# A fourth seven-product pair in the last two up chunks, and ten prepared pairs spread over seven chunks

## The chip, the cores and the metric

One core of one Trainium2 chip runs the whole layer in one launch. The metric is device time in microseconds (us), the median of several executions. TensorE is called PE here, VectorE DVE, ScalarE ACT, GpSimd POOL; SP is SyncE, which in this kernel only issues DMAs.

## The reference

A decoder layer for 256 tokens of width 2048, in float32. The last third of it is what the change touches:

```python
h = _rmsnorm(x, norm_mlp_pre[layer])
u = jnp.square(jax.nn.relu(h @ w_up[layer]))          # 2048 -> 8192
x = x + _rmsnorm(u @ w_down[layer], norm_mlp_post[layer])   # 8192 -> 2048
```

Ahead of it stand an input projection, two kinds of causal attention and an output projection.

## The kernel before

**Three matmuls for a product.** Every float32 operand is split in two parts: ACT writes `hi`, the value rounded to the type in which PE multiplies, and DVE writes `lo`, what is left (`lo = raw - hi`). A product is three matmuls of 128 rows by 512 columns: hi by hi, lo by hi, hi by lo. Weights come from HBM into a ring of five `raw` buffers (SP issues those DMAs), are split there into a ring of eight `hi` and eight `lo` buffers, and are consumed in the order in which they were planned; a split is written into each engine's program 7 tiles ahead of its use on PE.

**Chunks and steps.** `h @ w_up` runs in eight chunks `j` = 0 to 7 of 1024 columns. The table `UP_STEPS` lists the steps of a chunk. `k8` is a plain step: one tile of 128 rows of the weight, for both blocks of 128 tokens and both halves of 512 columns, 4 products or 12 matmuls. `w1` and `p2` take a pair of such tiles at once (pair 1 is k2 and k3) by Strassen's scheme in Winograd's form, with seven products, 21 matmuls, where two plain steps have eight products, 24 matmuls. For that, sums of the weight's four quarters are needed (`t` and `u`) and sums of the left operand's quarters (`s`, one set for a pair, the same for all chunks; the list `sums`).
- In a `w` step DVE makes `t` and `u` (three instructions, L360, L364, L365) from `ab`, a buffer of two tiles that GpSimd's queue fills (L378). They stand in DVE's program two tiles ahead of the pair's own splits. There is one buffer `ab`. In chunk 7, `w` pairs after the first load through `raw` instead (`raw_w`).
- In a `p` step the two sums were made beforehand by DMAs that add in HBM (`prepare`, ten pairs, early in the program); they are read back through the buffer `tu` by GpSimd's queue (chunks 1 to 4) or as two more `raw` tiles by SP (later chunks). DVE makes no sums there.

**Left sums.** `left_sums` makes `s` of pairs 0 to 3 during chunk 0. Pairs 0 to 2 are kept in `st`; pair 3 in `st2`, whose memory becomes `uT10` at the end of chunk 5. So chunks 1 to 5 use four pairs, chunks 6 and 7 three.

**The end of a chunk.** Seven products fill the four sums of a chunk (`acc_u`) and four more banks (`m1`, `m6`, `m7`, `m5`). After the last pair, `close` combines those into the four quarters of `c`: one ACT instruction (L1086), four on DVE (L1089). Two plain steps (k14, k15) follow on PE. Then, for each of the four quarters, `up_evac` adds `c` to `acc_u` on DVE (L979), ACT writes `r = relu(...)` (L983), PE transposes `r` in four pieces (`rt`, L301) and ACT squares the result into `uT` (L1001). The instruction streams are recorded in the order in which a planned clock (`Flow`) reaches them; the numbers behind `yield` are waits on that planned clock. So the yields in `up_evac` set behind how many matmuls of the next chunk the transposes stand in PE's program, which PE runs in order. "The end of chunk 3" is this sequence for chunk 3; its transposes stand among the matmuls of chunk 4.

After chunk 7 come two chunks of `u @ w_down`, mostly of the same two kinds of steps. They use `c` as a second load buffer.

Of the kernel before, what the change touches and what calls it, by code (L numbers as in the profile page):

```python
# [18 lines left out]
F32 = mybir.dt.float32  # L19
F32R = mybir.dt.float32r  # L20
# [6 lines left out]
P = 128  # L27
# [18 lines left out]
CW = 1024  # L46
# [51 lines left out]
NUP = FF // CW  # L98


def steps_of(text):

    return [(s[0], int(s[1:])) for s in text.split()]


UP_STEPS = {0: [("k", k) for k in range(KD)]}
for _j in range(1, 6):
    UP_STEPS[_j] = steps_of("k8 k9 k10 k11 p0 k12 w1 k13 p2 w3 k14 k15")
for _j in range(6, NUP):
    UP_STEPS[_j] = steps_of("k6 k7 k8 k9 k10 w0 k11 k12 w1 k13 w2 k14 k15")  # L110
SCALED = {j: range(8) for j in range(1, NUP)}
PREP = [(j, k) for j in UP_STEPS for w, k in UP_STEPS[j] if w == "p"]
D_PREP = (50.0, 24.0, 12.0)
# [151 lines left out]
def layer(nc, tc, io):  # L265
# [9 lines left out]
    dram = tc.alloc_tile_pool(name="dram", bufs=1, space=bass.MemoryType.DRAM)  # L275
# [69 lines left out]
    late = {}  # L345
# [599 lines left out]
    for ns in ((0, 1), (2,), (3,)):  # L945
# [4 lines left out]
        for c, b, acc in proj(mixT, [ch_o[n] for n in ns], f"o{ns[0]}", order, heads_done):  # L950
            n = ns[c]
# [23 lines left out]
    def up_evac(j, b, i, acc, order, more=None):  # L975

        if more is not None:
            yield 0.2
            nc.vector.tensor_tensor(out=acc, in0=acc, in1=more, op=OP.add)  # L979
            yield 1.8 if 4 <= j < 10 else 2.4  # L980
        yield UP_STEP * order
        r = late["up"].tile([P, 512], F32, tag="r", bufs=2, name=f"r{j}_{b}")
        nc.scalar.activation(r, acc, AF.Relu, scale=rstd2[b])  # L983
        yield D_UP if j > 1 else 2 * D_UP
        t = bank(i, f"rt{j}_{b}")
        for k in range(4):
            transpose(t[:, k * P:(k + 1) * P], r[:, k * P:(k + 1) * P])
        if j not in uT:
            if j in (12, 13):
                t2 = late["ab"][:, (j - 12) * CW:(j - 11) * CW]  # L990
            elif j in (8, 9):
                if j == 8:
                    late["uT8"] = late["up"].tile([P, 2 * CW], F32, tag="uT8", bufs=1, name="uT8")
                t2 = late["uT8"][:, (j - 8) * CW:(j - 7) * CW]
            elif j == 10:
                t2 = late["up"].tile([P, CW], F32, tag="uT10", bufs=1, name="uT10")
            else:
                tag = {"tag": "T", "bufs": 2} if j > 13 else {}
                t2 = late["up"].tile([P, CW], F32, name=f"uT{j}", **tag)
            uT[j] = t2.rearrange("p (k s) -> p k s", k=4)  # L1000
        nc.scalar.activation(uT[j][:, :, b * P:(b + 1) * P], t.rearrange("p (k s) -> p k s", k=4), AF.Square)  # L1001
# [29 lines left out]
        tt(out=qs[:, 3], in0=fs[:, 2], in1=qs[:, 2], op=OP.subtract)  # L1031

    sums = []

    def left_sums(kp):

        up, k, tt = late["up"], 2 * kp, nc.vector.tensor_tensor
        f, q = [late["c"][:, i * 512:(i + 1) * 512] for i in (2 * (kp % 2), 2 * (kp % 2) + 1)]
        hs = [t[:, k:k + 2, :].rearrange("p k s -> p (k s)") for t in hT]
        cuts = [(slice(i * S, (i + 1) * S), gcol[:, 8 + k + i:9 + k + i]) for i in range(2)]  # L1040
        for c, g in cuts:
            nc.scalar.activation(f[:, c], hs[0][:, c].bitcast(F32), AF.Copy, scale=g)
        yield 1.5
        for c, g in cuts:
            nc.vector.scalar_tensor_tensor(out=f[:, c], in0=hs[1][:, c].bitcast(F32), scalar=g, in1=f[:, c],
                                           op0=OP.mult, op1=OP.add)
        four_sums(q, f)
        sp, i0 = (late["st"], 2 * kp) if kp < 3 else (late["st2"], 2 * kp - 6)
        st = [sp[:, i * 512:(i + 1) * 512] for i in (i0, i0 + 1)]
        yield 3.0  # L1050
        for t, x in ((hs, f), (st, q)):
            nc.scalar.activation(t[0], x, AF.Copy)
        yield 1.5
        for t, x in ((hs, f), (st, q)):
            tt(out=t[1], in0=x, in1=t[0].bitcast(F32), op=OP.subtract)
        sums.append([[t[:, i * P:(i + 1) * P] for t in st] for i in range(4)])
        yield 0.5

    def some_sums(kps, after=0.0):
        yield after  # L1060
        for kp in kps:
            yield from left_sums(kp)
# [29 lines left out]
    def closing():  # L1092
        return [late["c"][:, i * 512:(i + 1) * 512] for i in range(4)]
# [3 lines left out]
    for j in range(FF // CW):  # L1097
# [9 lines left out]
        for t, b in order:  # L1107
            what, k, tiles = steps[t]
            if (j, t, b) == (0, 8, 0):
                flow.finish(*res)  # L1110
                late["po"].release()
                mix.release()
                late["up"] = pool("up", "right")
                late["st"] = late["up"].tile([P, 3 * CW], F32R, tag="st", bufs=1, name="st")
                for n in ("ab", "c"):
                    late[n] = late["up"].tile([P, 2 * CW], F32, name=n)
                late["st2"] = late["up"].tile([P, CW], F32R, tag="uT10", bufs=1, name="st2")
                late["tu"] = late["up"].tile([P, 2 * CW], F32, tag="uT8", bufs=1, name="tu")
                flow.start(some_sums((0, 1)))
                flow.start(some_sums((2, 3), 18.0))  # L1120
            if (j, t, b) == (FF // CW - 1, 4, 0):
                weights.limit -= 1
                u_next = split_u(0, 0)
            if what != "k":
                flow.until(lambda: len(sums) > k)
            if what == "k":
                w = weights.get(tiles[0])
                h_done(k, b)
                for n in range(2):
                    c = slice(n * 512, (n + 1) * 512)  # L1130
                    three(accs[b, n], [tok(hT[x], k, b) for x in range(2)], [w[x][:, 0, c] for x in range(2)], t == 0, t == len(steps) - 1)
                    if t == len(steps) - 1:
                        evac.append(flow.start(up_evac(2 * j + n, b, at[b, n], accs[b, n], 0.75 * (2 * b + n),
                                                       more[b, n] if j else None)))
                    flow.pump()
                if b == NB - 1:
                    weights.free(tiles[0])
                continue

            pairs = [s[1] for s in steps if s[0] != "k"]  # L1140
            first, last = k == pairs[0], k == pairs[-1]
            if first:
                m = {n: bank(i, f"m{n}_{j}") for n, i in zip((1, 6, 7, 5), free)}
            blocks = [[tok(hT[x], 2 * k + kk, bb) for x in range(2)] for kk, bb in ((0, 0), (1, 0), (1, 1))]
            seven_products(tiles, (blocks, sums[k]), accs, m, first, last)
            if last:
                more = close(closing(), m)
        free = [at[bn] for bn in PARTS]
    u_last = evac[-4:]
    up = late["up"]  # L1150
# [212 lines left out]
```

## Time and profile before

| | |
|---|---|
| median of 3 runs | 1045.58 us (1045.51 to 1045.67) |
| the profiled execution | 1045.31 us, of which the span is 1043.4 us |
| PE | busy 1033.9 us, 99% of the span; 99% of the chain that ended last |
| DVE, ACT, POOL | busy 79%, 61%, 10% |
| granted PE clock | 0.998 |
| up chunks 1 to 7 | about 400 to 701 us of the span |

The span is counted from the first to the last instruction; 1.9 us lie around it. A busy PE in this profile says that matmuls follow each other, and not at which rate; the rate is read from the starts of the matmuls. In a timeline each row is a start, a length, an engine, a line, the operation with its output and inputs, and in brackets how long the engine was idle before it and what ended that.

### The profile page before, as it was taken

How to read it: one execution, taken by the hardware profiler on the slowest of the kernel's cores; microseconds unless marked ns; L12 is line 12 of the kernel's file. 1: busy time of each engine (PE TensorE's matmuls, PEld its weight loads, DVE VectorE, ACT ScalarE, POOL GpSimd, SP SyncE). 2: the span in 40 equal slices, each digit the busy share in tenths (PEclk: the TensorE clock that was granted, in tenths of full speed). 3: DMA queues.
4: the chain of work that ended last, by engine and by line, in shares of the span. 5: the costliest groups of instructions: out<-in, count | busy, mean ns of one | idle time of the engine just before them, and what ended most of it. 6: DMA issues, size and time to landing. Idle time of an engine off the chain costs nothing.

```text
span 1043.4 us, 13587 instructions
## 1 busy us (share of the span) xinstructions
PE 1033.9 (99%) x4832; PEld 862.2 (83%) x4832; DVE 820.7 (79%) x1096; ACT 640.3 (61%) x862; POOL 103.8 (10%) x165
## 2 busy tenths in 40 slices
PE   9999999999999999999999999999999999999996
PEld 7888889888888888888888888888888888888885
DVE  7766537567547669988889788888999899999994
ACT  7674436565445558666766666666667566766761
POOL 0011111112001010010100000000000001112100
PEclk9999999999999999999999999999999999999999
DMA  9999879699878286756766666468888859789962
GB/s 337 353 300 281 211 202 320 203 251 295 238 217 262 95 343 215 270 204 232 264 210 235 211 216 198 152 223 296 300 275 310 284 185 334 263 306 321 365 220 81
DMA packets 93716, 262.90 MB, mean 252 GB/s; under 512 B 8785, under 2 KB 12881, under 8 KB 92241
## 3 DMA queue, kind: packets, MB, share of 16 engines
q1 hardware_dynamic: 70480, 187.99, 52.1%
q0 software_dynamic: 22304, 72.89, 24.5%
q10 hardware_dynamic: 864, 1.16, 0.3%
q8 instruction: 38, 0.62, 0.2%
q14 instruction: 30, 0.24, 0.1%
HBM read 245.22 MB, written 40.37 MB: 274 GB/s over the span
## 4 chain that ended last, share of the span: by engine, by line
PE 99%; DMA 0%; DVE 0%; ACT 0%; DVEq 0%; POOL 0%; issue 0%; ACTq 0%
PE acc_u L297 25%; PE y L297 25%; PE acc_o L297 8%; PE m L297 7%; PE md L297 6%; PE acc_qk L297 4%; PE acc_v L297 4%; PE acc_ckv L297 2%; PE acc_ukv L297 2%; PE acc_q L297 2%; PE acc_cq L297 2%; PE acc_k L297 2%; PE acc_uq L297 2%; PE rt L301 1%; PE y L1237 1%; PE sc_b L297 1%
## 5 line engine op out<-in xcount | busy, mean ns | idle before, releaser
L308 DVE TENSOR_TENSOR lo<-raw,hi 128x1024 fp32r<-128x1024 f32 (+3 forms) x234 | 262.0, 1137 | 86.6 <-ACT hi L307 85.5
L307 ACT ACTIVATE hi<-raw 128x1024 fp32r<-128x1024 f32 (+3 forms) x234 | 228.2, 988 | 83.9 <-DMA raw<-in_w_in 16.0
L297 PE MATMUL acc_u<-hi,hT_hi 128*128 128x512 f32 x356 | 141.8, 398 | 0.0
L297 PE MATMUL y<-hi,uhi 128*128 128x512 f32 x358 | 139.8, 391 | 0.0
L297 PE MATMUL y<-hi,ulo 128*128 128x512 f32 x358 | 139.5, 390 | 0.0
L297 PE MATMUL y<-lo,uhi 128*128 128x512 f32 x358 | 139.5, 390 | 0.0
L297 PE MATMUL acc_u<-hi,hT_lo 128*128 128x512 f32 x356 | 139.3, 391 | 0.0
L297 PE MATMUL acc_u<-lo,hT_hi 128*128 128x512 f32 x356 | 139.0, 391 | 0.0
L312 DVE SCALAR_TENSOR_TENSOR lo<-raw,gcol,hi 128x1024 fp32r<-128x1024 f32 x72 | 90.7, 1281 | 17.8 <-ACT hi L311 17.6
L311 ACT ACTIVATE hi<-raw,gcol 128x1024 fp32r<-128x1024 f32 x72 | 81.9, 1149 | 20.9 <-DMA raw<-in_w_up 12.9
L297 PEld LDWEIGHTS y<-hi,ulo 128*128 128x128 f32 x358 | 67.2, 188 | 14.1
L297 PEld LDWEIGHTS y<-lo,uhi 128*128 128x128 f32 x358 | 67.3, 188 | 13.8
L297 PEld LDWEIGHTS acc_u<-hi,hT_lo 128*128 128x128 f32 x356 | 66.8, 188 | 14.3 <-DVE hT_lo L308 0.2
L297 PEld LDWEIGHTS y<-hi,uhi 128*128 128x128 f32 x358 | 67.2, 188 | 13.7
L297 PEld LDWEIGHTS acc_u<-lo,hT_hi 128*128 128x128 f32 x356 | 67.0, 188 | 13.0
L297 PEld LDWEIGHTS acc_u<-hi,hT_hi 128*128 128x128 f32 x356 | 67.0, 188 | 12.8
L297 PE MATMUL m<-hi,st 128*128 128x512 f32 x156 | 56.5, 390 | 0.0
L308 DVE TENSOR_TENSOR lo<-st_down,hi 128x1024 fp32r<-128x1024 f32 x46 | 55.1, 1219 | 0.8 <-ACT hi L307 0.8
L297 PE MATMUL acc_o<-hi,mixT_hi 128*128 128x512 f32 x128 | 51.9, 405 | 0.0
L307 ACT ACTIVATE hi<-st_down 128x1024 fp32r<-128x1024 f32 x46 | 48.2, 1051 | 5.7 <-PE y L297 5.1
L297 PE MATMUL acc_o<-hi,mixT_lo 128*128 128x512 f32 x128 | 50.2, 393 | 0.0
L297 PE MATMUL acc_o<-lo,mixT_hi 128*128 128x512 f32 x128 | 50.0, 391 | 0.0
(341 smaller groups left out, 2093.4 us busy)
## 6 DMA issues: line engine op xcount, KB each, us to landing
raw<-in_w_up SPq DMA_DIRECT2D x86, 512.0 KB, 4.6
raw<-in_w_down SPq DMA_DIRECT2D x82, 512.0 KB, 5.7
raw<-in_w_in SPq DMA_DIRECT2D x55, 512.0 KB, 7.0
raw<-in_w_out SPq DMA_DIRECT2D x32, 512.0 KB, 7.4
ab<-in_w_up POOLq DMA_DIRECT2D x28, 512.0 KB, 5.1
ab_down<-in_w_down POOLq DMA_DIRECT2D x24, 512.0 KB, 7.2
sums<-in_w_up SPq DMA_DIRECT2D x20, 512.0 KB, 6.9
tu<-sums POOLq DMA_DIRECT2D x8, 1024.0 KB, 5.3
```

The source lines that it names most:

```text
L297: nc.tensor.matmul(out, a, b, start=start, stop=stop)
L301: nc.tensor.transpose(out, a, ident)
L307: nc.scalar.activation(hi, src, AF.Copy)
L308: nc.vector.tensor_tensor(out=lo, in0=src, in1=hi.bitcast(F32), op=OP.subtract)
L311: nc.scalar.activation(hi, src, AF.Copy, scale=g)
L312: nc.vector.scalar_tensor_tensor(out=lo, in0=src, scalar=g, in1=hi.bitcast(F32), op0=OP.mult, op1=OP.subtract)
L1237: nc.tensor.matmul(out, a[x], w[z], start=False, stop=(x, z) == (1, 0), skip_group_check=True)
```

## The change

1. `UP_STEPS`: chunks 4 and 5 have `w0` where they had `p0`. Chunks 6 and 7 had plain steps k6 and k7 and pairs `w0 w1 w2`; now they have the same list as chunks 4 and 5, with four pairs `w0 w1 p2 w3`. So there are 28 pairs instead of 26, and still ten prepared ones: two in each of chunks 1 to 3 and one in each of chunks 4 to 7.
2. The left sums of pair 3 are written to HBM (`st_kept`) by GpSimd's queue after they are made, and in chunks 6 and 7 read back by SP's queue before the step k11 into the memory of `c`, which is free between the last addition of one chunk and the `close` of its own. `c` becomes a tile with a tag, taken anew for each of these uses.
3. In `up_evac` the wait before `r` is 3.2 instead of 2.4 for the two halves of chunk 7.

```diff
-for _j in range(1, 6):
+for _j in range(1, 4):
     UP_STEPS[_j] = steps_of("k8 k9 k10 k11 p0 k12 w1 k13 p2 w3 k14 k15")
-for _j in range(6, NUP):
-    UP_STEPS[_j] = steps_of("k6 k7 k8 k9 k10 w0 k11 k12 w1 k13 w2 k14 k15")
+for _j in range(4, NUP):
+    UP_STEPS[_j] = steps_of("k8 k9 k10 k11 w0 k12 w1 k13 p2 w3 k14 k15")
...
-            yield 1.8 if 4 <= j < 10 else 2.4
+            yield 1.8 if 4 <= j < 10 else 3.2 if j > 13 else 2.4
...
+    st_kept = dram.tile([P, CW], F32, name="st_kept")
+
+    def new_c(name, dt=F32):
+        return late["up"].tile([P, 2 * CW], dt, tag="c", bufs=1, name=name)
+
+    def parts_of(st):
+        return [[st[:, w * 512 + i * P:w * 512 + (i + 1) * P] for w in range(2)] for i in range(4)]
...
+        if kp == 3:
+            yield 8.0
+            nc.gpsimd.dma_start(out=st_kept, in_=sp.bitcast(F32))
...
+            if j > 5 and (t, b) == (3, 0):
+                late["st2"] = new_c(f"st2_{j}", F32R)
+                nc.sync.dma_start(out=late["st2"][:, :CW].bitcast(F32), in_=st_kept)
+                sums[3] = parts_of(late["st2"])
...
             if last:
+                if j > 5:
+                    late["c"] = new_c(f"c_{j}")
                 more = close(closing(), m)
```

In `up_evac`, `j` counts halves of 512 columns: 4 to 9 are chunks 2 to 4, 14 and 15 chunk 7.

The program moves as follows at three places. First, DVE's program at the end of chunk 3, before; `lo207` to `lo212` are the splits of k14 and k15 of chunk 3 and of k8 to k11 of chunk 4, `lo213` and `lo214` those of the first two tiles of chunk 4's pair 0.

```order
L312 SCALAR_TENSOR_TENSOR lo210_4789<-raw210_4786,gcol_69,hi210_4788 128x1024
L312 SCALAR_TENSOR_TENSOR lo211_4801<-raw211_4798,gcol_69,hi211_4800 128x1024
L312 SCALAR_TENSOR_TENSOR lo212_4813<-raw212_4810,gcol_69,hi212_4812 128x1024
L1089 TENSOR_TENSOR c_3574<-m6_3_4613,c_3574 128x512
L1089 TENSOR_TENSOR c_3574<-m7_3_4614,c_3574 128x512
L1089 TENSOR_TENSOR c_3574<-m5_3_4615,c_3574 128x512
L1089 TENSOR_TENSOR c_3574<-c_3574,m7_3_4614 128x512
L308 TENSOR_TENSOR lo213_4832<-raw213_4829,hi213_4831 128x512
L308 TENSOR_TENSOR lo214_4850<-raw214_4847,hi214_4849 128x1024
L979 TENSOR_TENSOR acc_u3_00_4501<-acc_u3_00_4501,c_3574 128x512
```

The same place after the change (the lines of the file are 10 further down from `close` on).

```order
L312 SCALAR_TENSOR_TENSOR lo210_4792<-raw210_4789,gcol_69,hi210_4791 128x1024
L360 TENSOR_TENSOR t4_0_4801<-ab_3574 128x1024
L364 TENSOR_TENSOR u4_0_4802<-t4_0_4801,ab_3574 128x512
L365 TENSOR_TENSOR u4_0_4802<-u4_0_4802,ab_3574 128x512
L312 SCALAR_TENSOR_TENSOR lo211_4809<-raw211_4806,gcol_69,hi211_4808 128x1024
L312 SCALAR_TENSOR_TENSOR lo212_4821<-raw212_4818,gcol_69,hi212_4820 128x1024
L1099 TENSOR_TENSOR c_3575<-m6_3_4615,c_3575 128x512
L1099 TENSOR_TENSOR c_3575<-m7_3_4616,c_3575 128x512
L1099 TENSOR_TENSOR c_3575<-m5_3_4617,c_3575 128x512
L1099 TENSOR_TENSOR c_3575<-c_3575,m7_3_4616 128x512
L308 TENSOR_TENSOR lo213_4836<-ab_3574,hi213_4835 128x512
L308 TENSOR_TENSOR lo214_4852<-ab_3574,hi214_4851 128x1024
```

The three instructions that make the sums of chunk 4's pair 0 now stand ahead of chunk 3's `close` and first addition; the same happens at the end of chunk 4. At the ends of chunks 5 and 6 they stood there already.

Second, PE's program where the first transposes of chunk 3 stand, before.

```order
L297 MATMUL acc_u4_10_4870<-hi209_4779,hT_lo_2923 128x512
L297 MATMUL acc_u4_11_4871<-hi209_4779,hT_hi_2922 128x512
L297 MATMUL acc_u4_11_4871<-lo209_4780,hT_hi_2922 128x512
L297 MATMUL acc_u4_11_4871<-hi209_4779,hT_lo_2923 128x512
L301 MATMUL rt6_0_4891<-ident_94,r6_0_4880 128x128 x4
L297 MATMUL acc_u4_00_4868<-hi210_4788,hT_hi_2922 128x512
```

And after.

```order
L297 MATMUL acc_u4_10_4872<-hi209_4782,hT_lo_2923 128x512
L297 MATMUL acc_u4_11_4873<-hi209_4782,hT_hi_2922 128x512
L297 MATMUL acc_u4_11_4873<-lo209_4783,hT_hi_2922 128x512
L297 MATMUL acc_u4_11_4873<-hi209_4782,hT_lo_2923 128x512
L301 MATMUL rt6_0_4895<-ident_94,r6_0_4884 128x128 x4
L297 MATMUL acc_u4_00_4870<-hi210_4791,hT_hi_2922 128x512
```

They stand behind the 12 matmuls of k8 in both. The same holds at the end of chunk 4 (12 and 12); at the ends of chunks 5 and 6 it is 15 and 15, at the end of chunk 7 it was 15 and is 18. PE's whole program has six matmuls fewer.

Third, SP's program in chunk 6 after the change: `raw265` is k12, `raw270` k13, `raw271` to `raw274` the four tiles of the prepared pair 2.

```order
L189 DMA raw260_5558<-in_w_up 128x1024
L189 DMA raw265_5674<-in_w_up 128x1024
L1132 DMA st2_6_5700<-st_kept_3328 128x1024
L189 DMA raw270_5757<-in_w_up 128x1024
L189 DMA raw271_5769<-in_w_up 128x512
L189 DMA raw272_5787<-in_w_up 128x1024
L189 DMA raw273_5801<-sums6_2_78 128x1024
L189 DMA raw274_5813<-sums6_2_78 128x1024
```

The new load stands in the middle of the weights' queue, which it did not have before; in chunk 7 it stands likewise between the loads of k12 and k13.

More of the change, by code (lines that the diff above doesn't have):

```diff
@@ L1114, in layer @@
                 late["st"] = late["up"].tile([P, 3 * CW], F32R, tag="st", bufs=1, name="st")
-                for n in ("ab", "c"):
-                    late[n] = late["up"].tile([P, 2 * CW], F32, name=n)
+                late["ab"], late["c"] = late["up"].tile([P, 2 * CW], F32, name="ab"), new_c("c")
                 late["st2"] = late["up"].tile([P, CW], F32R, tag="uT10", bufs=1, name="st2")
```

## The prediction

> **What bounds the kernel now.** I read the page's totals first, then the chain that ended last, then the timelines of DVE, ACT and PE around the ends of chunks, since only there does PE wait for a result that is made late. The totals and the chain's shares:
>
> ```profile
> PE 1033.9 (99%) x4832; PEld 862.2 (83%) x4832; DVE 820.7 (79%) x1096; ACT 640.3 (61%) x862; POOL 103.8 (10%) x165
> ...
> PE 99%; DMA 0%; DVE 0%; ACT 0%; DVEq 0%; POOL 0%; issue 0%; ACTq 0%
> ```
>
> PE is the chain from start to end. So time changes in two ways only: by the number of matmuls on PE, and by stalls of PE that come or go. The chain in order of time, at the ends of chunks 3, 4 and 5 (start, length, what):
>
> ```profile
> 523.19 8.16 PE acc_u L297 x36
> ...
> 565.92 8.16 PE acc_u L297 x36
> 574.09 0.44 PE rt L301 x4
> 574.52 2.09 PE acc_u L297 x9
> ...
> 608.66 8.84 PE acc_u L297 x39
> 617.50 0.50 PE rt L301 x4
> 618.00 2.08 PE acc_u L297 x9
> ```
>
> The 36 matmuls behind a chunk's last pair (24 of k14 and k15, 12 of the next chunk's first step) take 8.16 us without a gap: 0.2267 us each. At the end of chunk 5 there are 39, and the four transposes take 0.50 instead of 0.44: PE waited 0.06 us for `r` there. At the other ends shown it did not. How near `r` came is in the timelines. DVE at the end of chunk 3:
>
> ```profile
> 514.86 1.23 DVE L308 TENSOR_TENSOR lo<-t,hi 128x1024 fp32r<-128x1024 f32 x1 [1.30 <-ACT hi L307]
> 516.00 6.13 DVE L312 SCALAR_TENSOR_TENSOR lo<-raw,gcol,hi 128x1024 fp32r<-128x1024 f32 x5
> 522.36 1.28 DVE L312 SCALAR_TENSOR_TENSOR lo<-raw,gcol,hi 128x1024 fp32r<-128x1024 f32 x1 [0.22 <-ACT hi L311]
> 523.56 2.28 DVE L1089 TENSOR_TENSOR c<-m,c 128x512 f32<-128x512 f32 x3
> 525.87 0.69 DVE L1089 TENSOR_TENSOR c<-c,m 128x512 f32<-128x512 f32 x1
> 526.48 1.82 DVE L308 TENSOR_TENSOR lo<-raw,hi 128x512 fp32r<-128x512 f32 x2
> 528.21 1.89 DVE L979 TENSOR_TENSOR acc_u<-acc_u,c 128x512 f32<-128x512 f32 x3
> ```
>
> At 514.86 DVE had waited for ACT, so it held no backlog. From there it works through six splits, the close and two splits to the first addition at 528.21. ACT and PE at the same place:
>
> ```profile
> 528.94 0.69 ACT L983 ACTIVATE r<-acc_u,rstd_pre 128x512 f32<-128x512 f32 x1 [1.93 <-DVE acc_u L979]
> ...
> 531.19 0.60 PE L301 MATMUL rt<-ident,r 128*128 128x128 f32 x4
> ```
>
> `r` ends at 529.63, the transposes' turn on PE comes at 531.19: 1.56 us to spare.
>
> **The matmuls removed.** Two pairs (one each in chunks 6 and 7) go from two plain steps, 24 matmuls, to seven products, 21: six fewer, at 0.2267 us 1.36 us less. All of it lies on the chain. The trace knows no other price for a matmul in this stage, so this term has hardly a range.
>
> **The sums ahead of the close, chunks 3 and 4.** Because chunks 4 and 5 now begin with `w0`, DVE makes its sums ahead of the close. Their price stands where the same three instructions run now, for pair 1 of chunk 4:
>
> ```profile
> 531.74 1.22 DVE L360 TENSOR_TENSOR t<-ab 128x1024 f32<-128x1024 f32 x1
> 532.99 0.69 DVE L364 TENSOR_TENSOR u<-t,ab 128x512 f32<-128x512 f32 x1
> 533.72 0.69 DVE L365 TENSOR_TENSOR u<-u,ab 128x512 f32<-128x512 f32 x1
> 534.33 1.22 DVE L308 TENSOR_TENSOR lo<-tu,hi 128x1024 fp32r<-128x1024 f32 x1
> ```
>
> From 531.74 to 534.33 they hold DVE for 2.59 us, more than the 1.56 us to spare. What the whole sequence then takes shows at the end of chunk 5, which has these sums ahead of the close already:
>
> ```profile
> 600.33 1.23 DVE L308 TENSOR_TENSOR lo<-t,hi 128x1024 fp32r<-128x1024 f32 x1 [1.30 <-ACT hi L307]
> ...
> 607.37 1.22 DVE L360 TENSOR_TENSOR t<-ab 128x1024 f32<-128x1024 f32 x1
> ...
> 611.15 2.28 DVE L1089 TENSOR_TENSOR c<-m,c 128x512 f32<-128x512 f32 x3
> ...
> 615.87 1.89 DVE L979 TENSOR_TENSOR acc_u<-acc_u,c 128x512 f32<-128x512 f32 x3
> ...
> 616.60 0.69 ACT L983 ACTIVATE r<-acc_u,rstd_pre 128x512 f32<-128x512 f32 x1 [4.12 <-DVE acc_u L979]
> ...
> 617.34 0.66 PE L301 MATMUL rt<-ident,r 128*128 128x128 f32 x4
> ```
>
> From the start of the last pair's `lo<-t` at 600.33 to the transposes at 617.34 it is 17.01 us, and 17.07 with the 0.06 that they were late. That row has the same idle time before it (1.30, ended by ACT) as the row at 514.86, so both begin without a backlog. Applied to chunk 3: 514.86 + 17.07 = 531.93, while PE arrives at 531.19: PE stalls 0.74 us. At the end of chunk 4:
>
> ```profile
> 557.59 1.23 DVE L308 TENSOR_TENSOR lo<-t,hi 128x1024 fp32r<-128x1024 f32 x1 [1.30 <-ACT hi L307]
> ...
> 572.08 0.67 ACT L983 ACTIVATE r<-acc_u,rstd_pre 128x512 f32<-128x512 f32 x1
> ...
> 573.93 0.60 PE L301 MATMUL rt<-ident,r 128*128 128x128 f32 x4
> ```
>
> 557.59 + 17.07 = 574.66 against 573.93: 0.73 us. The difference from chunk 5 is the place of the transposes: there 15 matmuls of the next chunk precede them, here 12, and three matmuls are 0.68 us. The three later quarters of each end move along, since each `r` waits for the buffer that the transposes before it release. Bounds for the two stalls together: nothing, if DVE regains the 2.59 us beforehand; at most 2.44 us, the 2.59 less the time to spare now, 1.56 at the end of chunk 3 and 1.18 at the end of chunk 4 (there `r` starts at 572.08, takes 0.67, and PE comes at 573.93; it starts late for another reason, a load that is no longer ahead of it). I take 1.47, because the rows of chunk 5 are the same sequence.
>
> On the price of the sums, the Trainium skill, page "VectorE: DVE Perf Modes", section "Mode 1× (REGULAR) — the baseline", says that such an addition yields one result a cycle, at 0.96 GHz. By that the 2048 results would take 2.13 us (an estimate from the page), each stall 0.46 us less, and the sum of all terms would be about -0.7 us. The rows' 2.59 us include what each instruction costs besides its results, and I use those.
>
> **Ends of chunks 5 and 6.** k8 and k9 are scaled by a gain (1.28 us a split) where k6 and k7 were not (1.22): `close` starts 0.12 later. Between close and first addition, splits of 0.69 and 1.22 stand in place of 1.28 and 0.69, 0.06 earlier. That leaves 0.06 us at each end, 0.12 together. In chunk 6 the close's first instruction, on ACT, must now wait until PE has read the left sums out of `c`, thus for the pair's end, about 608.7 in the chunk that I compare with, plus 0.6 for itself. DVE comes to the close at 611.15 only. So this wait is covered by DVE's backlog; without that cover it would cost what ACT's copy takes, 0.6 us.
>
> **End of chunk 7.** The copy waits likewise, and DVE has less backlog there. The transposes stand three matmuls, 0.68 us, later, which takes in the 0.6. I cost it at nothing, with 0 to 0.7 as bounds.
>
> **What else is added, and its cover.** DVE gains 2.59 us in chunks 4 and 5 each; in chunks 6 and 7 the sums of `w3` replace those of `w2`, and four splits of 0.69 + 3 × 1.22 replace two of 1.22, 1.9 us more. DVE's load in this stage:
>
> ```profile
> 550.00:600.00 50.00, 50.00 (x230) 41.39 (x229) 42.59 (x45) 33.10 (x39) 3.23 (x6) 1.00 0.66 218
> ...
> 650.00:700.00 50.00, 50.00 (x230) 41.28 (x229) 43.57 (x49) 31.61 (x36) 0.00 (x0) 1.00 0.54 179
> ```
>
> After the stretch and its length come the busy times of PE, PEld, DVE, ACT and POOL. DVE is busy 85 to 87%, so 6 to 7 us of 50 are free; ACT has more. The splits run ahead of PE; the least lead in chunks 2 to 7 is at k13 of chunk 6, the split and its first use on PE:
>
> ```profile
> 639.60 1.28 DVE L312 SCALAR_TENSOR_TENSOR lo<-raw,gcol,hi 128x1024 fp32r<-128x1024 f32 x1
> ...
> 644.69 0.39 PE L297 MATMUL acc_u<-lo,hT_hi 128*128 128x512 f32 x1
> ```
>
> That is 3.8 us, so the few us more of DVE's work in a chunk, spread over its idle times, do not reach PE. GpSimd's one store of 0.5 MB and the swapped loads of `ab` and `tu` are covered likewise: POOL is 6% busy in the first of these windows.
>
> SP's queue is the open point. The load of the left sums waits until `c` has been read by the last addition of the chunk before, and five loads for k13 and pair 2 wait behind it. In the rows of before, that addition and the times of the weights' loads between 640 and 705 us, from issue to landing, are:
>
> ```profile
> 618.80 0.69 DVE L979 TENSOR_TENSOR acc_u<-acc_u,c 128x512 f32<-128x512 f32 x1
> ...
> DMA to landing us min/median/max: 3.5/4.7/8.0
> ```
>
> `c` is free at 619.49, 5.6 us into chunk 6. k13 is preceded by k8 to k11, pair 0, k12 and pair 1: 60 + 42 matmuls, 23.1 us, and transposes of 1.8. Even at 8.0 us and with 2.5 us for the split it is ready 16.1 us into the chunk, 8.8 us before its use at 24.9. So nothing is charged.
>
> **The sum.** -1.36 + 0.74 + 0.73 + 0.12 = +0.23 us. The profiled execution took 1045.31 us, 1.91 of it outside the span, so it would take 1045.5; it lies 0.27 below the median of the runs. From the median 1045.58 it is 1045.8 us. The bound of a measurable change, 0.2%, is 2.1 us: above 1047.7 is slower, below 1043.5 faster.
>
> **Rivals.**
> - *The full gain.* DVE catches up before the ends of chunks 3 and 4, and PE does not stall. For it: the 1.30 us idle before `lo<-t`, and 0.22 more at the end of chunk 3. Against it: the idle time lies ahead of the sums, where it can't be used, and only the 0.22 behind. 1045.58 - 1.36 + 0.12 = 1044.3 us.
> - *Slower, by SP's queue.* The loads behind the one of the left sums come late in chunks 6 and 7, and the splits of k13 and pair 2 with them. For it: the burst is six loads, 2.75 MB, on a queue that has them spread out now, beside GpSimd's load for pair 1. Against it: the 8.8 us worked out above. It decides when k13 lands over 16.8 us after its issue (24.9 - 5.6 - 2.5), which is a little more than two loads of 8.0 us one after the other; at 18.8 us PE would wait 2 us in each of the two chunks: 1045.8 + 4 = 1049.8 us. On this the Trainium skill, page "DMA: Bandwidth & Descriptors", section "Queues, rings and completion order", says that each DMA engine takes turns between queues packet by packet, so GpSimd's transfers would take part of the rate from this burst. No row of before shows such a burst.
> - *The close comes late in chunks 6 and 7.* If ACT reaches the copy only after other work, all four quarters slip. Each end would stall by up to the copy's 0.6 plus a split on ACT of 1.1: 1045.8 + 2 × 0.85 (the middle) = 1047.5 us.
>
> That the matmuls are not removed is excluded by PE's program.
>
> **How the numbers follow.** My forecast, 1045.2 to 1046.5, has 0.58: the stalls are read off rows of the same sequence. The full gain or most of it, 1044.1 to 1045.2, has 0.25. The late close has 0.09, SP's queue 0.08. The range from 1044.1 takes in the full gain, and goes to 1047.2, which cuts off SP's queue and half of the late close. Slower is SP's queue and a part of the late close, 0.10; faster would need a gain beyond all six matmuls, 0.02; the same 0.88.
>
> **What would show it.** PE with 4826 matmuls; in the chain the transposes at the ends of chunks 3 and 4 at 1.1 to 1.2 us instead of 0.44, at the ends of chunks 5 and 6 at 0.5 to 0.6, at the end of chunk 7 at 0.44; `close` on DVE at the end of chunk 3 at about 525.9 instead of 523.56; in chunks 6 and 7 the first split of k13 waiting for no DMA. The prediction is wrong if the transposes at the ends of chunks 3 and 4 take 0.44, or if PE waits for a split in chunk 6 or 7.

## The result: 1.5 us slower, outside the predicted range

On one chip, the changed kernel took 1047.32 us (median of 20 runs, 1045.78 to 1048.72) and the kernel before 1045.82 us (20 runs, 1045.14 to 1046.74). The ratio is 1.0014, with a 95% interval of 1.0007 to 1.002: slower by 0.7 to 2.1 us, less than the 0.2% called measurable, but not nothing, and 0.12 us above the range. The profiled execution of the changed kernel took 1046.54 us, with a span of 1044.8 against 1043.4 before. It is 0.78 below the median of its kernel, so its rows can show less than a median run lost.

Totals and shares of the chain on the page of the changed kernel:

```profile
PE 1033.9 (99%) x4826; PEld 860.2 (82%) x4826; DVE 828.5 (79%) x1106; ACT 643.5 (62%) x866; POOL 106.3 (10%) x169
...
PE 98%; DVE 1%; ACT 0%; issue 0%; DVEq 0%; POOL 0%; ACTq 0%
```

The six matmuls are gone (4832 to 4826), yet DVE is now on the chain. Where, the chain in order of time says (start, length, what), at the ends of chunks 3 and 4:

```profile
523.41 3.41 PE acc_u L297 x15
526.85 0.70 DVE c L1099
...
529.58 1.22 DVE lo L308
531.45 0.70 ACT r L983
...
570.41 0.70 DVE c L1099
...
575.00 0.70 ACT r L983
```

Before, 36 matmuls ran here in one piece of 8.16 us, with the transposes right behind. Now the chain leaves PE after 15 of them and goes through `close`, a split, the addition and `r`: PE waits for `r`. The rows of DVE, ACT and PE at the end of chunk 3:

```profile
515.08 1.23 DVE L308 TENSOR_TENSOR lo<-t,hi 128x1024 fp32r<-128x1024 f32 x1 [1.30 <-ACT hi L307]
...
521.08 1.22 DVE L360 TENSOR_TENSOR t<-ab 128x1024 f32<-128x1024 f32 x1
...
523.67 2.47 DVE L312 SCALAR_TENSOR_TENSOR lo<-raw,gcol,hi 128x1024 fp32r<-128x1024 f32 x2
526.07 2.28 DVE L1099 TENSOR_TENSOR c<-m,c 128x512 f32<-128x512 f32 x3
...
531.45 0.69 ACT L983 ACTIVATE r<-acc_u,rstd_pre 128x512 f32<-128x512 f32 x1 [4.16 <-DVE acc_u L979]
...
532.19 0.66 PE L301 MATMUL rt<-ident,r 128*128 128x128 f32 x4 [0.61 <-ACT r L983]
```

The sums hold DVE from 521.08 to 523.67, 2.59 us; `close` begins at 526.07 where it began at 523.56. From `lo<-t` to the transposes it is 17.11 us, against 17.07 predicted. The last matmul ahead of the transposes starts at 531.18 and the next instruction could start 0.23 us later, the usual distance of two starts. So PE lost 0.77 us ahead of the transposes, and 0.06 in them: 0.83. At the end of chunk 4 the same rows lie 43.55 us later, again 0.83.

The end of chunk 7, DVE in the kernel before and then in the changed one:

```profile
693.06 3.49 DVE L308 TENSOR_TENSOR lo<-raw,hi 128x1024 fp32r<-128x1024 f32 x3
696.46 2.28 DVE L1089 TENSOR_TENSOR c<-m,c 128x512 f32<-128x512 f32 x3
...
701.65 1.89 DVE L979 TENSOR_TENSOR acc_u<-acc_u,c 128x512 f32<-128x512 f32 x3
```

```profile
693.26 1.23 DVE L308 TENSOR_TENSOR lo<-raw,hi 128x1024 fp32r<-128x1024 f32 x1 [0.61 <-ACT hi L307]
695.33 3.77 DVE L308 TENSOR_TENSOR lo<-raw,hi 128x1024 fp32r<-128x1024 f32 x3 [0.85 <-ACT hi L307]
699.02 2.13 DVE L1099 TENSOR_TENSOR c<-m,c 128x512 f32<-128x512 f32 x3
...
704.06 1.89 DVE L979 TENSOR_TENSOR acc_u<-acc_u,c 128x512 f32<-128x512 f32 x3
```

DVE was fully busy there; now it waits for ACT, and `close` starts 2.56 us later, the first addition 2.41. What ACT waits for from 660 to 704 us (total, times, longest), before and then changed:

```profile
ACT hi L307 <- PE acc_u L297: 9.0, 8, 2.1
...
ACT hi L307 <- DMA raw<-in_w_down: 1.8, 1, 1.8
```

```profile
ACT hi L307 <- DMA raw<-in_w_down: 4.4, 6, 1.5
...
ACT hi L307 <- PE acc_u L297: 2.4, 2, 2.1
...
ACT hi L307 <- DMA raw<-sums: 1.6, 2, 1.4
```

Before, ACT waited for PE to release `hi` buffers: the weights were early. Now it waits for the weights. Three of the four transposes of chunk 7 come late, by 0.14, 0.44 and 0.18 us, together about 0.75. The span's 1.3 us are then -1.36 (matmuls) + 1.66 (ends 3 and 4) + 0.04 (ends 5 and 6) + 0.75 (end of 7), and 0.24 by which the up stage already began later.

### The profile page after: what moved, and what is told of

Read it like the earlier page. It is cut to its first block, busy times and chain, and to the rows that moved or that the text cites. A ratio compares the mean times of both kernels' runs of the same rounds, so it can differ in the third digit from the quotient of the medians.

```text
span 1044.8 us, 13589 instructions
## 1 busy us (share of the span) xinstructions
PE 1033.9 (99%) x4826; PEld 860.2 (82%) x4826; DVE 828.5 (79%) x1106; ACT 643.5 (62%) x866; POOL 106.3 (10%) x169
## 4 chain that ended last, share of the span: by engine, by line
PE 98%; DVE 1%; ACT 0%; issue 0%; DVEq 0%; POOL 0%; ACTq 0%
PE y L297 25%; PE acc_u L297 23%; PE acc_o L297 8%; PE m L297 7%; PE md L297 6%; PE acc_qk L297 4%; PE acc_v L297 4%; PE acc_ckv L297 2%; PE acc_ukv L297 2%; PE acc_q L297 2%; PE acc_cq L297 2%; PE acc_k L297 2%; PE acc_uq L297 2%; PE rt L301 1%; PE y L1252 1%; PE sc_b L297 1%
## 5 line engine op out<-in xcount | busy, mean ns | idle before, releaser
L297 PE MATMUL acc_u<-hi,hT_hi 128*128 128x512 f32 x344 | 137.0, 398 | 0.0
L297 PE MATMUL acc_u<-hi,hT_lo 128*128 128x512 f32 x344 | 134.4, 391 | 0.0
L297 PE MATMUL acc_u<-lo,hT_hi 128*128 128x512 f32 x344 | 134.1, 390 | 0.0
L312 DVE SCALAR_TENSOR_TENSOR lo<-raw,gcol,hi 128x1024 fp32r<-128x1024 f32 x72 | 90.3, 1281 | 15.2 <-ACT hi L311 15.1
L297 PEld LDWEIGHTS acc_u<-hi,hT_lo 128*128 128x128 f32 x344 | 64.6, 188 | 13.9 <-DVE hT_lo L308 0.2
L297 PEld LDWEIGHTS acc_u<-lo,hT_hi 128*128 128x128 f32 x344 | 64.7, 188 | 12.5
L297 PEld LDWEIGHTS acc_u<-hi,hT_hi 128*128 128x128 f32 x344 | 64.7, 188 | 12.3
L297 PE MATMUL m<-hi,st 128*128 128x512 f32 x168 | 60.8, 389 | 0.0
```

The lines of the kernel that those rows point to most:

```text
L297: nc.tensor.matmul(out, a, b, start=start, stop=stop)
L312: nc.vector.scalar_tensor_tensor(out=lo, in0=src, scalar=g, in1=hi.bitcast(F32), op0=OP.mult, op1=OP.subtract)
```

## The experiments

Each kernel ran 11 times, next to 33 runs of the kernel before on the same chip (medians 1045.45, 1045.67 and 1045.67 us for the three groups of four). Differences below are to that median; their intervals are about 0.9 us to each side, and they can differ by up to 0.5 us from what the ratio says, which is not the ratio of these medians. For the changed kernel the difference is +1.50. "Waits" at an end are PE's, read off the starts of its matmuls.

### 1. Ends of chunks 3 and 4 behind 15 matmuls

```diff
-            yield 1.8 if 4 <= j < 10 else 3.2 if j > 13 else 2.4
+            yield 1.8 if 4 <= j < 6 else 3.2 if j > 13 else 2.4
```

> The changed kernel with the wait before r 2.4 instead of 1.8 at the ends of chunks 3 and 4, so that the transposes stand behind 15 matmuls of the next chunk instead of 12. Theory (the sums ahead of the close make r late at these two ends, 0.83 us of stall each in the profile after): the transposes' gap shrinks by 0.68 us at each end, to about 0.15; time 1.4 us below the changed kernel, within 0.3 us of the kernel before (it was 1.5 above). Rival (DVE is late there whatever the place, and the stall follows the transposes): no gain, 1.5 us above the kernel before.

1045.46 us, +0.0, ratio 0.9997 (0.9988 to 1.0006). Its chain:

```profile
524.46 8.84 PE acc_u L297 x39
533.30 0.59 PE rt L301 x4
```

39 matmuls in one piece; 0.15 us of each 0.83 stay. So the stalls at these ends come from what stands ahead of the transposes, and are worth about 1.4 us.

### 2. The kernel before, with only the sums moved into chunks 4 and 5

```diff
+for _j in range(4, 6):
+    UP_STEPS[_j] = steps_of("k8 k9 k10 k11 w0 k12 w1 k13 p2 w3 k14 k15")
```

> The kernel before with one part of the change alone: w0 instead of p0 in chunks 4 and 5 (eight prepared pairs instead of ten), chunks 6 and 7 as before; no matmul fewer. Theory: only the two stalls at the ends of chunks 3 and 4 are added, 0.83 us each: 1.5 to 1.7 us above the kernel before. Rival (the stalls need the rest of the change, or are made up for later): within 0.3 us of the kernel before.

1047.37 us, +1.9, ratio 1.0019 (1.001 to 1.0028): this part alone makes the kernel slower. Its chain at the end of chunk 3 is the changed kernel's, with 0.83 us of waits there and at the end of chunk 4, and no others that the kernel before doesn't have:

```profile
523.13 3.41 PE acc_u L299 x15
526.57 0.70 DVE c L1091
...
531.16 0.70 ACT r L985
```

### 3. No pair 3 in chunk 7

```diff
+UP_STEPS[7] = steps_of("k6 k7 k8 k9 k10 w0 k11 k12 w1 k13 p2 k14 k15")
...
-            if j > 5 and (t, b) == (3, 0):
+            if j == 6 and (t, b) == (3, 0):
```

> The changed kernel with pair 3 of chunk 7 undone: k6 and k7 plain again there, pairs w0 w1 p2, no load of the left sums in chunk 7; three matmuls more (+0.68 us). Theory (the fourth pair of chunk 7 loads its two weight tiles through the five raw buffers, so the loads of the first down tiles start late, the close of chunk 7 comes late and its transposes stall PE, 0.70 us in the profile after and more in slower runs): these stalls are gone, time between 0.0 and 0.5 us below the changed kernel, 1.0 to 1.5 above the kernel before, and the runs lie as close together as those before (1.6 us from lowest to highest instead of 2.9). Rival (the spread and the extra come from elsewhere): 0.7 us above the changed kernel, 2.2 above the kernel before, as widely spread.

1048.03 us (1046.50 to 1049.78), +2.6, ratio 1.0023 (1.0014 to 1.0031), with three matmuls more (+0.68): a miss, nearer to what the rival said. 0.6 us of waits stay at the end of chunk 7, without the fourth pair and without the load of left sums there. What stays is the prepared pair 2, and the later place of the transposes. The profile also has 1.2 us of waits at the end of chunk 1, which this edit doesn't touch.

### 4. Transposes of chunk 7 later still

```diff
-            yield 1.8 if 4 <= j < 10 else 3.2 if j > 13 else 2.4
+            yield 1.8 if 4 <= j < 10 else 5.2 if j > 13 else 2.4
```

> The changed kernel with the wait before r 5.2 instead of 3.2 at the end of chunk 7: the first transposes stand behind 30 matmuls of the down stage instead of 18, 2.7 us later. Theory (late r at the end of chunk 7 is the rest of the loss, and it varies from run to run): PE does not wait there; 0.7 to 1.2 us below the changed kernel, 0.3 to 0.8 above the kernel before, with a smaller spread. Rival (the loss that varies is a late weight in chunk 7, so PE waits for a split whatever the place of the transposes): no difference to the changed kernel, 1.5 above the kernel before, same spread.

1046.93 us, +1.5, ratio 1.0017 (1.0008 to 1.0026): nothing gained. The wait moved to a later transpose, and its chain shows where the time is made:

```profile
686.60 7.06 DMA raw<-in_w_down
...
694.85 1.24 DVE lo L308
...
696.11 5.71 DMA raw<-in_w_down
...
701.87 1.21 DVE lo L308
...
703.10 8.57 DMA raw<-in_w_down
...
711.77 1.06 ACT hi L307
```

A split frees a `raw` buffer, the load into it takes 6 to 9 us, ACT and DVE split it, and that frees the buffer again: the ring of five `raw` buffers is a loop on the chain. A later place on PE doesn't change it.

### 5. The store of the left sums later

```diff
-            yield 8.0
+            yield 80.0
             nc.gpsimd.dma_start(out=st_kept, in_=sp.bitcast(F32))
```

> The changed kernel, with GpSimd's store of the left sums issued later, behind its loads for chunk 1 instead of right behind their first. Theory (the store runs beside the weights' loads in chunk 1 and, in some executions, makes the end of chunk 1 late): the first transposes of chunk 1 have 0.5 us or more to spare again, as without the store (0.65), instead of 0.24; the time is 0.2 to 0.5 us below the changed kernel's, about 1046.9, and the spread of its runs shrinks towards that of the kernel before. Rival (the store costs nothing, the spread comes from elsewhere): no difference in time or spread. The stalls at the ends of chunks 3, 4 and 7 stay at 0.83, 0.83 and about 0.75 us by both.

1046.98 us (1046.28 to 1049.24), +1.3, ratio 1.0015 (1.0006 to 1.0023): neither the time nor the spread moved by what can be told. The spare time at the end of chunk 1, from the end of the first `r` to its transposes, was 0.54 us here. In the seven kernels with the late store it lies between 0.23 and 0.91, and PE waits there in none. With the early store it is 0.24 in the changed kernel and 0.57 in experiment 4; but in experiments 1, 3 and 6 PE waits there, for 0.03, 1.2 and 0.3 us. So the medians don't show that the store costs anything, and the profiles, one execution each, leave open that it does in some executions.

### 6. Chunk 7 with its old list

```diff
+UP_STEPS[7] = steps_of("k6 k7 k8 k9 k10 w0 k11 k12 w1 k13 w2 k14 k15")
...
-            if j > 5 and (t, b) == (3, 0):
+            if j == 6 and (t, b) == (3, 0):
```

> The changed kernel with the list that chunk 7 had before: two plain steps more and the pairs 0, 1 and 2 made by sums, no prepared pair and no load of left sums there; nine prepared pairs, three matmuls more. Theory (the prepared pair's four raw tiles in chunk 7, on SP's queue beside the first loads of w_down, make ACT's hi and with it the close late): the 0.75 us of stalls at the end of chunk 7 are gone, its first quarter is added at most 1 us behind the last matmul of the chunk instead of 2.5; with three matmuls more (+0.68) the time is that of the changed kernel within 0.2 us. Rival (the later place of the transposes, or anything else that stays, makes the end of chunk 7 late): the stalls stay at 0.6 to 0.9 us and the time is 0.7 us above the changed kernel's.

1046.80 us, +1.1, ratio 1.0014 (1.0005 to 1.0022). With three matmuls more than the changed kernel it is not slower than that. Of the 0.75 us at the end of chunk 7, 0.18 stay, at the fourth transpose; the first has 1.84 us to spare with the transposes still behind 18 matmuls. So the place is not the cause; the new list of chunk 7 is.

### 7. All ends late, and the store late

```diff
-            yield 1.8 if 4 <= j < 10 else 3.2 if j > 13 else 2.4
+            yield 1.8 if 4 <= j < 6 else 3.2 if j > 5 else 2.4
```

and the store as in experiment 5.

> The changed kernel with the transposes behind 18 matmuls at the ends of chunks 3 to 6, as at the end of chunk 7, and the store of the left sums issued later. Theory (only stalls at the ends of chunks stood against the six matmuls): no stall at the ends of chunks 3 to 6, against 0.83, 0.83 and 0.15 us; 0.75 us stays at the end of chunk 7. So -1.36 + 0.75 - 0.12 = -0.7 against the kernel before, 0.5 to 0.9 us below it, and 2.0 to 2.4 us below the changed kernel. Rival (the stalls move to the later quarters of an end or to the next chunk's splits, as when the transposes of chunk 7 were put later): within 0.3 us of the kernel before.

1046.46 us, +0.8, ratio 1.0005 (0.9996 to 1.0014). The ends of chunks 3 to 6 have no wait left, and `u @ w_down` begins at 700.00 us, 1.36 earlier than in the changed kernel. But the first pair of that stage begins at nearly the same time as there (731.15 against 731.26): between the two, where chunk 7's transposes stand, it takes 2.06 us more than in the kernel before, where the changed kernel took 0.81 more. The theory had counted on 0.75 and on a time below the kernel before: a miss. The up stage began 0.36 us later here. Counted from its start, 0.47 of the 1.73 us gained at the ends of chunks 3 to 6 are left at that pair; in experiment 1 it was 1.13 of 1.35, and by the medians the gain is 0.7 us here (+0.8 against +1.5) and 1.5 there. So a part of what is gained ahead of the end of chunk 7 comes back as a longer wait there, a large part in this profile and a small one in that of experiment 1.

### 8. The prepared pair early in chunk 7

The kernel of experiment 7 with

```diff
+UP_STEPS[7] = steps_of("k8 k9 k10 k11 w0 p2 k12 w1 k13 w3 k14 k15")
```

> The kernel with late transposes and late store, and in chunk 7 the prepared pair 2 stands third from the front of the pairs' order, behind pair 0, instead of ahead of the last pair; its four raw tiles are then loaded before the first loads of w_down. Theory (those four tiles beside the loads of w_down make the end of chunk 7 late): the stalls at the end of chunk 7 shrink from 0.75 to at most 0.2 us, and the time is 1.0 to 1.4 us below the kernel before, 0.5 to 0.7 below the same kernel with the old order. Rival (the number of loads in the chunk decides, not their place, or pair 2 comes too early for its splits): no gain over the old order, or a wait of PE for a split of pair 2 in chunk 7.

1047.90 us, +2.2, ratio 1.0022 (1.0013 to 1.0031): a miss. The number of loads is the same, and those of `w_down` left later than in experiment 7 (first at 687.1 against 685.2 us); PE waits 1.4 us for a split of `w_down` ahead of the first transposes.

### 9. The load of left sums further back in SP's queue

In the changed kernel SP's queue stands still in chunk 7 until `c` is free. What SP's queue waits for from 640 to 704 us:

```profile
...
SPq L1132 <- DVE acc_u L979: 12.7, 1, 12.7
```

The kernel of experiment 7 with

```diff
-            if j > 5 and (t, b) == (3, 0):
+            if j > 5 and (t, b) == (6, 0):
```

> The kernel with late transposes at the ends of chunks 3 to 6 and the late store, and in chunks 6 and 7 the load of the left sums stands two loads later on SP's queue, behind the tiles of k13 and the first of pair 2. Theory (in chunk 7 the load of the left sums stands first in the queue and waits until c is free, at about 663 us, while the buffers of the two loads behind it are free at about 655 and 659; all loads after it lose that lead): the two loads are issued before 660 us, PE's waits at the end of chunk 7, 2.0 us in the same kernel without this edit, shrink to at most 0.75, and the time is about 1.3 us below that kernel, some 0.5 below the kernel before. Rival (the number of loads alone makes the end of chunk 7 late): no difference to the kernel without this edit.

1046.28 us, +0.6, ratio 1.0006 (0.9997 to 1.0015). The two loads were issued at 654.4 and 655.6 us instead of 663.5 and 664.0, as expected, and the end of chunk 7 took 1.94 us more than before instead of 2.06; the theory had at most 0.75. At its later place the load still held the queue for 7.7 us, where it was 12.7. So the shorter wait gained next to nothing. The chain still runs through the ring:

```profile
690.74 1.29 DVE lo L312
692.04 5.29 DMA raw<-in_w_down
...
698.53 1.22 DVE lo L308
699.75 0.61 DVE c L1099
```

### 10. The load of left sums on GpSimd's queue

The kernel of experiment 7 with

```diff
-                nc.sync.dma_start(out=late["st2"][:, :CW].bitcast(F32), in_=st_kept)
+                nc.gpsimd.dma_start(out=late["st2"][:, :CW].bitcast(F32), in_=st_kept)
```

> As with the load two places later, but here it is issued by GpSimd's queue at its old place, and SP's queue doesn't have it at all. Theory (the wait at the front of SP's queue): PE's waits at the end of chunk 7 shrink from 2.0 to at most 0.75 us, the time is about 1.3 us below the kernel with SP's load, within 0.3 of the one with the load later on SP. Rival (number of loads alone): no difference to the kernel with SP's load; a third way, the load on GpSimd's queue makes the first loads of c or ab for w_down late, would show as waits of DVE or ACT for those.

1046.68 us, +1.0, ratio 1.0008 (0.9999 to 1.0017): no gain over experiment 7 either, though SP's queue doesn't wait for `c` at all. The profiled execution is the fastest of the eleven (1044.60), so the smaller loss at its end of chunk 7 (1.06 us) doesn't speak for the others.

### 11. Nine prepared pairs, chunk 7 as before, late ends

The kernel of experiment 7 with the list and the condition of experiment 6.

> Late transposes at the ends of chunks 3 to 6, late store, and chunk 7 with its old list: no prepared pair and no load of left sums there, three matmuls more. Theory (the prepared pair's loads and the waiting load make the end of chunk 7 late): PE's waits at the end of chunk 7 are 0.2 us or less, none at the other ends; -0.68 - 0.12 + 0.2 = 0.6 us below the kernel before. Rival (the later transposes of chunk 6 make chunk 7 late by themselves): waits of 1 us or more at the end of chunk 7 and no gain.

1044.71 us (1044.40 to 1045.80), -1.0, ratio 0.9995 (0.9986 to 1.0004). It beats the changed kernel, whose ratio is 1.0014 (1.0007 to 1.002); against the kernel before the interval takes in no change. Experiment 7 differs from it in the list of chunk 7 alone, with the load that goes with it, and took 1.75 us more by the medians, with three matmuls fewer. Its chain at the end of chunk 7 never leaves PE:

```profile
694.71 5.44 PE acc_u L298 x24
700.15 4.08 PE y L298 x18
704.23 0.44 PE rt L302 x4
...
712.47 0.62 PE rt L302 x4
```

0.18 us at the fourth transpose is all that is left. The transposes of chunk 6 are as late as in experiment 7, so they aren't what made its end of chunk 7 late.

### 12. Four pairs in chunk 7, none prepared

The kernel of experiment 9 with

```diff
+UP_STEPS[7] = steps_of("k8 k9 k10 k11 w0 k12 w1 k13 w2 w3 k14 k15")
```

> As the kernel with the load two places later, and in chunk 7 pair 2 is made by sums on DVE instead of prepared: four seven-product pairs, two raw tiles fewer, 2.6 us more of DVE. Theory (the waiting load and the two additional raw tiles are all that makes the end of chunk 7 late): PE's waits there are 0.3 us or less, and with all six matmuls gone the time is about 1.1 us below the kernel before. Rival (DVE is the limit in chunk 7 once the loads are early): the sums take the place of the loads, waits of 0.5 to 1.5 us stay, and the time is within 0.4 us of the kernel before.

1046.21 us, +0.5, ratio 1.0007 (0.9999 to 1.0016): a miss, and about what the rival said. DVE from 680 to 690 us in this kernel, in the kernel before and in the changed one (after the stretch and its length, the busy times of PE, PEld, DVE, ACT), and what ACT waits for in this kernel:

```profile
680.00:690.00 10.00, 10.00 (x45) 8.28 (x45) 9.96 (x13) 5.97 (x7) 0.00 (x0) 1.00 0.60 197
```

```profile
680.00:690.00 10.00, 10.00 (x46) 8.28 (x45) 8.60 (x10) 6.01 (x6) 0.00 (x0) 1.00 0.47 157
```

```profile
680.00:690.00 10.00, 10.00 (x45) 8.28 (x45) 9.75 (x11) 6.94 (x8) 0.00 (x0) 1.00 0.71 222
```

```profile
ACT hi L308 <- DMA raw<-in_w_down: 4.4, 4, 2.8
...
ACT hi L308 <- DVE u L366: 3.5, 2, 3.2
```

DVE is full, and the splits that free the buffers come late: the first load of `w_down` leaves as early as before, but the second at 687.6 us, 5.4 behind it; in the kernel before it is 0.6 behind. The sums have taken the place of the two loads; that they are why nothing was gained is read off these rows, and no run tests it. In the changed kernel DVE was nearly as full in this stretch (9.75 of 10 us, against 8.60 before), so its work isn't excluded there as a part of the cause.

## Why the prediction was wrong

**Right: the matmuls.** 4826 on PE; with every end of chunks 3 to 6 free of waits, `u @ w_down` began 1.42 us earlier, counted from the start of the up stage (experiment 7), against six times 0.2267, 1.36, and the 0.12 that the kernel before lost at the ends of chunks 5 and 6.

**Right: the mechanism at the ends of chunks 3 and 4; the size a little off.** 1.66 us measured, 1.47 predicted. The sequence on DVE took 17.11 us against 17.07 applied; the rest is that transposes which wait also take 0.06 longer. Experiments 1 and 2 take this term away and put it alone. The bound from below, "nothing, if DVE regains the 2.59 us beforehand", and with it the full gain as a rival, are refuted. The price of the sums held at the rows' 2.59 us. The 2.13 us estimated from one result a cycle (Trainium skill, page "VectorE: DVE Perf Modes", section "Mode 1× (REGULAR) — the baseline") count the results alone. The trace has 1.22 us for 1024 results and 0.69 for 512, some 0.15 us more for each instruction; by the estimate each stall would have been 0.46 shorter, and it was not.

**Right enough: ends of chunks 5 and 6.** 0.04 us together against 0.12; the copy of `c` in chunk 6 was covered.

**Wrong: the end of chunk 7, costed at nothing.** It cost 0.75 us in the profile, just over the bound of 0.7. By the medians it was more: the changed kernel is 0.37 us above experiment 6, which has three matmuls (0.68) more, so the new list cost about 1.1 us between the two, with an interval of about 1 us, where their profiles show 0.6. I counted there only the copy's wait for `c` and three matmuls more of time. What I didn't count is that the new list sends more tiles through SP's queue and the five `raw` buffers ahead of `w_down`: 16 tiles and the left sums in chunk 7, where it was 14 tiles (a prepared pair has four, a pair made by sums two, a plain step one; pair 0 comes through `ab`). In chunk 6 the same list ended on time: there GpSimd's queue loads all pairs made by sums, and 12 tiles and the left sums pass. The loads of weights and sums from 660 to 704 us, kernel before and then changed (count, first and last issue):

```profile
L189 SPq DMA_DIRECT2D raw<-in_w_down x11: 327/328/328, 682.6 to 701.8; - x11
L189 SPq DMA_DIRECT2D raw<-in_w_up x3: 328/328/328, 673.5 to 676.2; - x3
L189 SPq DMA_DIRECT2D raw_w<-in_w_up x1: 328/328/328, 671.1 to 671.1; - x1
```

```profile
L189 SPq DMA_DIRECT2D raw<-in_w_down x10: 327/328/328, 686.3 to 703.0; - x10
L189 SPq DMA_DIRECT2D raw<-in_w_up x5: 327/333/430, 664.6 to 685.1; - x5
L189 SPq DMA_DIRECT2D raw_w<-in_w_up x2: 328/328/328, 670.2 to 674.2; - x2
L189 SPq DMA_DIRECT2D raw<-sums x2: 327/327/327, 677.7 to 678.3; - x2
DMA to landing us min/median/max: 3.5/5.2/8.2
```

15 tiles before, 19 after. One turn of a buffer is a load of 5.2 us (median), ACT's 1.1 and DVE's 1.2: 7.5 us without any wait between them, so by this estimate five buffers pass a tile each 1.5 us at best. From the first load of `w_down` on it is 1.9 us a tile in both kernels, so there is little to catch up with, and that first load left 3.7 us later than before. Measured against the first matmul of `u @ w_down`, and beside what the stretch up to that stage's first pair took more than in the kernel before:

| kernel | first load of `w_down` ahead of its stage, us | stretch, us more |
|---|---|---|
| before | 18.2 | 0 |
| experiment 2, sums moved only | 18.2 | 0.00 |
| experiment 6, old list | 18.2 | 0.23 |
| experiment 11, old list, late ends | 18.2 | 0.24 |
| experiment 3, pair 2 prepared, no pair 3 | 15.1 | 0.65 |
| changed | 15.1 | 0.81 |
| experiment 5, store late | 15.1 | 0.81 |
| experiment 1, late ends of 3 and 4 | 15.1 | 1.03 |
| experiment 4, later transposes | 15.1 | 1.07 |
| experiment 7, late ends | 14.8 | 2.06 |
| experiment 10, load by GpSimd | 14.7 | 1.06 |
| experiment 9, load further back | 14.1 | 1.94 |
| experiment 8, pair 2 early | 12.9 | 3.46 |
| experiment 12, no prepared pair | 18.0 | 3.24 |

The lead tells the kernels with the old list from most of those with the new one, but it doesn't measure the loss: experiments 7 and 10 have the same lead and differ by 1.0 us, and experiment 12 lost most but one at nearly the old lead and with 14 tiles, as before, beside the left sums; there DVE was full.

And the step "the few us more of DVE's work in a chunk, spread over its idle times, do not reach PE" looked at the lead of the splits before their own matmuls. That lead did hold in the changed kernel; what came late was `close`, which stands behind those splits on DVE.

**The rivals.** SP's queue was the wrong place: its wait of 12.7 us was there in chunk 7, but moving the load (experiments 9 and 10) changed nothing that can be told, and in chunk 6 k13 was ready 7.4 us before its use. The cover of 8.8 us was worked out on chunk 6 alone, so it could not show what comes late in chunk 7. The Trainium skill, page "DMA: Bandwidth & Descriptors", section "Queues, rings and completion order", has each DMA engine take turns between queues. No run here separates that from the length of the ring. The late close came nearest, with 1047.5 us: it happened in chunk 7 and not in chunk 6, but behind late splits, not by ACT's order, and I had given it 0.09.

**The rest.** The sum, corrected, is -1.36 + 1.66 + 0.04 + 0.75 = +1.1 us, and the kernel before was 0.24 us slower on the chip of the comparison than in the runs the prediction starts from: 1045.82 + 1.1 = 1046.9, inside the range. The measured 1047.32 is 0.4 above that. The 1.1 us that the medians give for the end of chunk 7, in place of 0.75, would cover it, but their interval is wider than the 0.4, so this stays open. The runs of the kernels with the new list in chunk 7 scatter over 2.1 to 4.3 us, those of experiment 11 over 1.4 and those of experiment 2 over 1.8, both with the old one; a loop of loads that differ from run to run would do that, but the profile shows one execution each, so this stays an explanation that was only argued. Experiment 6, without those loads at the end of chunk 7, scattered as widely (1046.05 to 1049.58), which speaks against it as the only reason; it has the early store, and in its profile PE waits 0.3 us at the end of chunk 1.

**What is shown, and what isn't.** That the new list of chunk 7 makes its end late, and not the place of the transposes, is shown by experiments 6 and 11. What in that list does it is argued. That the ring of `raw` buffers is the loop is read off the chains of experiments 4 and 9, and a kernel with a sixth buffer was not tried. DVE's fuller stretch (experiment 12) may be a part of the cause, and so may the rate of the DMAs: between 690 and 700 us the DMA engines were busy for 0.91 of the time in the changed kernel and for 0.74 before. No run takes these apart.

## What to carry to other kernels

Where one engine is the whole chain, a saving on it can be lost in part at the next point that is paced by something else (of 1.73 us, 0.47 were left in experiment 7; of 1.35, 1.13 in experiment 1). Find that point first, and count the tiles that pass its buffers in the same time, before and after. A price that is read off the same sequence elsewhere in the trace can be close (17.07 us predicted, 17.11 measured); a term costed at nothing needs the same search for a row. The lead of an operand before its own use doesn't cover what stands behind it in its engine's program.

## What was not expected of the hardware

- The same load of 128x1024 from `w_down` took 5.3 to 8.6 us from the release of its buffer to its landing where the ring was on the chain (experiments 4 and 9).
- A wait at the front of SP's queue that fell from 12.7 to 7.7 us gained next to nothing: 0.12 us between the profiles of experiments 7 and 9, and 0.2 between their medians.
- Between executions, a kernel's time scattered by 3.0 to 3.6 us (experiments 5, 7, 12) or by 1.4 (experiment 11), at a granted clock of 0.997 to 0.999 in every run.
